# Long convolutions' first stage as two 64-row matmuls into neighbouring banks, PSUM as four banks and two pairs, gates stored by 128 channels

## The chip, the cores and the metric

The kernel runs on one core of one Trainium2 chip. A core has five engines with an instruction queue each: TensorE (PE, matrix products), VectorE (DVE), ScalarE (ACT), GpSimd (POOL) and SyncE (SP, which here only issues transfers). Products land in PSUM, a small memory of 8 banks; one bank takes 512 float32 values in each of 128 partitions. DVE and ACT read PSUM. Everything else lies in SBUF (on the core) or in DRAM. The metric is the device time of one execution in microseconds, the median of several runs.

## The reference, cut to what matters

One layer over 2048 tokens of width 1024: a projection, half of whose columns go through a Fourier mix and half through a gated long convolution, then an output projection, then a two-layer product with a squared ReLU. The change edits the long convolutions and how PSUM is dealt out to all stages.

```
p   = rmsnorm(x) @ w_in            # 512 Fourier columns, 3 x 512: x1, x2, v
y_f = rmsnorm(Re(FFT2(fourier columns)))
x1, x2, v = short_conv(...)        # three taps along the tokens
z = v
for n, gate in enumerate((x1, x2)):
    z = gate * irfft(rfft(z, 4096) * k_freq[n], 4096)[:2048]  (+ z * long_d[n])
x = x + concat(y_f, rmsnorm(z)) @ w_out
x = x + relu(rmsnorm(x) @ w_fc1)**2 @ w_fc2
out = rmsnorm(x)
```

## The kernel before, in words

The stages follow each other, with a small overlap at the seams.

**Projection** (`project`, L308, in two passes, about 0 to 220 and 220 to 425 us). The first pass makes the gates x1 and x2, the second the Fourier columns and v. For each of 16 token tiles there are two products of 24 matmuls (three per weight tile: each float32 operand is split into a high and a low part, `mm3`, L187), into PSUM tiles `pu0` and `pu1`. DVE and POOL apply the three taps, and `finish` (L392) stores a 128 x 512 tile of a gate in the DRAM array `gates`, laid out [128, 16, 512], one piece of 2 KB per partition. Beside the first pass run `filter_hidden` and `fourier_weights`.

**Fourier mix and filters** (L421 and L471, about 425 to 644 us). DFTs as matmuls; the filters' spectra are stored in DRAM as `spec`.

**Long convolutions** (`hyena`, L606, about 644 to 872 us). Eight blocks: two convolutions of four groups of 128 channels. A 4096-point transform is written as two stages of matmuls with a transpose between them. For a block:
- `first(c)` (L636), eight calls for 16 channels each: two matmuls with 256 columns into one PSUM bank `pz1`. The moving operand zz is [128 rows, 16, 16 channels]; the stationary e1 has two matrices, one per half sp. The e1 matrix of half sp is zero in the 64 rows of the other half. DVE then transposes the bank (128 x 512) into G (`turned`, L416).
- `second(q)` (L645), eight slots q: four matmuls of 128 x 128 into `pz2`. ACT makes a turned copy zs of it, DVE multiplies it by the spectrum (y, L655), POOL multiplies zs by the spectrum (L656), and y and zs are added on POOL or DVE (L657). The spectrum `ks` comes by two transfers of 256 KB per slot (L628), into four buffers.
- `inverse(q)` (L660), three slots later: four matmuls of 128 x 128 with y as the stationary operand, into `pv`; ACT copies it to V.
- `turn(c)` (L668): DVE transposes V into W.
- `gate(q)` (L673), four calls: two matmuls whose outputs are the two halves of one bank's partitions (`pb`), and DVE multiplies it by the gate xg into zz (L679). xg of a block is one transfer of 1 MB (`load`, L619) from `gates`.

A hand-written table sets the order over the slots of block i: `second(q)`; at q = 1 the four gates of block i - 2; the last three inverses and the turns of block i - 1; `inverse(q - 3)`; at q = 3 the load of xg for block i - 1; and at the end of a slot the calls of `first` for block i + 1, by the table `FIRSTS` (two in slots 0 and 1, one in slots 2 to 5). All eight calls for block 0 come ahead of the loop.

**Output projection** (`project_out`, L791, to about 1070 us), **first product** (`fc1`, L994, to about 1725 us) and **second product** (`fc2`, L1110, to the end). The last two use a scheme of seven products m1 to m7 instead of eight; `p1u`, `p1m`, `p1v` and `p2u`, `p2m`, `p2v` are their PSUM tiles. In `fc2`, u, m and v are four tiles each, for four groups of 128 tokens; a group of 14 steps is repeated four times for each of two token blocks, and u lives through a whole group.

**PSUM.** All stages take tiles of one bank from `pa` (L165), eight buffers under one tag. A tile's buffer is given out again when every reader of the tile is done. The framework orders the instructions of every engine from the program's order, priorities and an estimate of durations at compile time, and adds the waits; on the chip each engine's order is fixed.

Of the kernel before, what the change touches and what calls it, by code (L numbers as in the profile page):

```python
# [10 lines left out]
F32 = mybir.dt.float32  # L11
# [116 lines left out]
P = 128  # L128
# [6 lines left out]
def hybrid_block(ctx: ExitStack, tc: tile.TileContext, A, out):  # L135
# [7 lines left out]

    gd = [scratch(f"gates{i}", [P, NT, 512]) for i in range(3)]
    kd = [[scratch(f"spec{i}{n}", [P, 32, 128]) for n in range(2)] for i in range(4)]
# [16 lines left out]
    def pool(name, side="left"):  # L162
        return tc.tile_pool(name=name, bufs=1, side=side, reuse_waits="tile")

    def pa(nm):  # L165
        return ps.tile([P, 512], F32, tag="a", name=nm, bufs=8)

# [51 lines left out]
    def transposed(src, nm):  # L219

        for b in (0, 4):
            pt = pa(f"pt_{nm}")
# [7 lines left out]
    def fourier_weights(wp):  # L230

        yield
        rd = load(wp, "rd", [P, P], A["rdft"])
        wt = {}
        for k in range(9):
            if k < 8:
                t = load(wp, "wf", [P, 512], A["w_in"][128 * k : 128 * k + 128, 0:512], 2)
                p = pa("pwt")
                for c in range(4):
                    nc.tensor.transpose(p[:, 128 * c : 128 * c + 128], t[:, 128 * c : 128 * c + 128], ident)  # L240
                wt[k] = wp.tile([P, 4, 128], F32, tag="wt", name="wt", bufs=2)
                nc.scalar.copy(wt[k], p.rearrange("p (c d) -> p c d", c=4))
            if k:
                p = pa("pwr")
                for c in range(4):
                    nc.tensor.matmul(p[:, 128 * c : 128 * c + 128], lhsT=wt[k - 1][:, c, :], rhs=rd, start=True, stop=True)
                wr = wp.tile([P, 512], F32, tag="wr", name="wr", bufs=2)
                nc.scalar.mul(wr, p, gmix[:, k - 1 : k])
                nc.sync.dma_start(wfd[128 * k - 128 : 128 * k, :], wr)
            yield  # L250


    def filter_hidden(fh):

        yield
        w0 = load(fh, "w0", [66, P], A["filt_w0"])
        wi = load(fh, "wi", [P, 2, P], A["filt_wi"])
        fb = load(fh, "fb", [P, 4], A["filt_bf"])
        for half in range(2):
            cur = {}  # L260
            for layer in range(3):
                for q in (2 * half, 2 * half + 1):
                    if layer == 0:
                        cur[q] = load(fh, "feat", [66, 512], A["feat"][:, 512 * q : 512 * q + 512], 2)
                    p = pa(f"ph{layer}")
# [42 lines left out]
    def project(ip, fx, cps, sets, uf):  # L308
# [36 lines left out]
        for i, t in enumerate(order):  # L345
            xh, xl = ahead
            if w is None:
# [9 lines left out]
                if uf is None:  # L357
                    norm(15, xts[15])
            r = rx[t]
            for h, s in enumerate(sets):  # L360
                p = pa(f"pu{h}")
                for k in range(8):
# [29 lines left out]
                def finish(acc, m, tt):  # L392
                    nc.vector.tensor_add(acc, acc, m)
                    nc.sync.dma_start(gd[s][:, tt, :], acc)

# [19 lines left out]

    def turned(dst, c, src):  # L416

        nc.vector.transpose(dst.rearrange("p c f e -> p c e f")[:, 8 * c : 8 * c + 8], src)

# [186 lines left out]
    def hyena(hp, wp, rp, zz, e1, b1, f2, a2, out_weights, out_ahead):  # L606
# [6 lines left out]
        class Block:  # L613
# [5 lines left out]
            def load(self):  # L619
                self.xg = hp.tile([P, NT, 128], F32, tag="xg", name="xg", bufs=2)  # L620
                nc.sync.dma_start(self.xg, gd[1 + self.n][:, :, self.cs])

# [13 lines left out]
            def first(self, c):  # L636
                if c == 0:
                    self.G = big("G")
                p = pa("pz1")
                lo = 128 * self.ct + 16 * c  # L640
                for sp in range(2):
                    nc.tensor.matmul(p[:, 256 * sp : 256 * sp + 256], lhsT=e1[:, sp, :], rhs=zz[:, :, lo : lo + 16], start=True, stop=True)
                turned(self.G, c, p.rearrange("p (l c e) -> p c e l", c=8, e=2))

            def second(self, q):  # L645
                ks = self.ahead if q == 0 and self.ahead else self.spectrum(q)
                p = pa("pz2")
                for j in range(4):
# [11 lines left out]
            def inverse(self, q):  # L660
                if q == 0:
                    self.V = big("V")
                p = pa("pv")
                for j in range(4):
# [8 lines left out]
            def gate(self, q):  # L673
                p = pa("pb")
                for sp in range(2):
# [9 lines left out]
        LAST = ((0,), (1, 2), (3, 4), (5, 6), (7,))  # L685
        FIRSTS = ((0, 1), (2, 3), (4,), (5,), (6,), (7,), (), ())
        blocks = [Block(n, ct) for n in range(2) for ct in range(4)]
        for c in range(8):
            blocks[0].first(c)
# [42 lines left out]
    class Out:  # L732
# [24 lines left out]
        def parts(self, yn, yh, yl, t=0):  # L757

            pt = pa("pt_y")
            for k in range(4):  # L760
# [11 lines left out]
        def ahead(self, hp):  # L772
# [11 lines left out]
            for t, f in zip(tokens, fronts):  # L784
                self.begun[t] = [pa("po") for _ in range(2)]
                for h in range(2):
# [4 lines left out]
    def project_out(op, work, rp, b):  # L791
# [27 lines left out]
        def back(t, f, z):  # L819
            xt = op.tile([P, 1024], F32, tag="oxt", name="oxt", bufs=2)  # L820
            nc.sync.dma_start(xt, x_t[:, t, :])
            x2 = op.tile([P, 1024], F32, tag="ox2", name="ox2", bufs=2)
            for h in range(2):
                if f:
                    p = pa("po")
                    work.multiply(p, f, 0, h)
                else:
                    p = work.begun[t][h]
                cols = slice(512 * h, 512 * h + 512)
# [29 lines left out]
        for i in range(NT + 1):  # L859
# [17 lines left out]
            else:  # L877

                begun = [pa("p1u"), pa("p1m")]
                for p, n in zip(begun, ("m1", "m2")):  # L880
# [22 lines left out]
        for n in ("m5", "m6"):  # L903
            fc1_split(b, n, nc.gpsimd)
        begun.append(pa("p1v"))
        begun.extend([pa("p1u"), pa("p1m")])
        fc1_product(begun[3], ahead["m1"], b["m1"], True)
# [86 lines left out]
    def fc1(mp, rp, zp, b, first, following, begun):  # L994
# [64 lines left out]
        for i in range(33):  # L1059
# [6 lines left out]
            if i < 32:  # L1066
                a = nxt
                if i < 31:
                    nxt = weights(*(fc1_weights(rp, (i + 1) % 16, 1 - i % 2) if i else following), i + 1)
                pu, pm = (pa("p1u"), pa("p1m")) if i > 1 else begun[3 * i : 3 * i + 2]  # L1070
                use(pu, a, "m1", True, i)
# [13 lines left out]
            if i < 32:  # L1085
                use(pu, a, "m6", False, i)
                with tc.high_priority(offset=0 if i else 400):
                    u2 = keep(pu, "ku2")
                pv = pa("p1v") if i else begun[2]
                use(pv, a, "m5", True, i)  # L1090
# [7 lines left out]
        for i, n in enumerate(("m1", "m2")):  # L1098
            parts = []
            for j, v in enumerate(fc2_rows(0, n, 0)):  # L1100
# [3 lines left out]
                split(*parts[j], t)  # L1104
            fc2_begun[n] = [pa("p2" + "um"[i]) for _ in range(4)]
            for j, p in enumerate(fc2_begun[n]):
# [3 lines left out]
    def fc2(mp, blk, gfin, begun):  # L1110
# [64 lines left out]
        def use(k, j):  # L1175
            g, n, e = steps[k]
            bank, start, (rows, cols) = todo[n]
            if k in parts:
                if start and e == 0:
                    held[bank, j] = pa(f"p2{bank}")  # L1180
                fc2_product(held[bank, j], j, *parts[k], start and e == 0)
# [195 lines left out]
```

## Time and profile before

| | |
|---|---|
| median of 3 runs | 2336.13 us (2333.21 to 2342.69) |
| the profiled execution's own time | 2342.11 us |
| its span, from the first to the last instruction | 2340.2 us |
| mean granted TensorE clock | 0.986 |
| PE busy, whole span | 2247.7 us |
| stretch 0 to 220 us (first projection pass): PE busy | 209.02 us |
| 220 to 425 (second pass): PE busy | 191.45 us |
| 425 to 644 (Fourier mix, filters): PE busy, DVE busy | 196.12 us, 186.80 us |
| 644 to 872 (long convolutions): PE busy, DVE busy, DMA share | 211.54 us, 173.16 us, 0.89 |
| 872 to 1070 (output projection): PE busy | 195.08 us |
| 1070 to 1725 (first product): PE busy | 638.77 us |
| 1725 to 2340 (second product): PE busy, DVE busy | 605.74 us, 427.36 us |

"Busy" is the time in which an engine runs at least one instruction. The ends of matmuls are modelled, so a busy PE need not be at its peak. A row of a timeline gives start, duration, engine, line, operation, output tile and input tiles, and how many records were merged; a float32 matmul leaves two records, since it is run in two passes. In brackets stands the idle time before it, and who ended it. "DMA share" is the mean busy share of the core's 16 DMA engines; a value a little over 1 means that packets overlap on an engine.

### The profile page before, as it was taken

To read this page: it belongs to the slowest core of one execution; us is meant where nothing else is said; L and a number is where in the kernel's file an instruction comes from. 1 tells how busy PE (TensorE), PEld (TensorE's weight loads), DVE (VectorE), ACT (ScalarE), POOL (GpSimd) and SP (SyncE) were. 2 spreads that over 40 slices of the span, in tenths; PEclk is the share of its full clock that TensorE was granted. 3 is DMA by queue.
4 is the path that set the end of the run, shared out by engine and by line. 5 is a ranking of instruction groups with operands and counts; after the bars stand their busy time and mean duration, and the time that the engine had idled before them with its cause. 6 is when DMAs were issued, how large, how long until landed. Compare 5 with 4: busy or idle time off the path is not lost.

```text
span 2340.2 us, 30973 instructions
## 1 busy us (share of the span) xinstructions
PE 2247.7 (96%) x10984; PEld 1861.0 (80%) x10984; DVE 1548.4 (66%) x2284; ACT 1104.3 (47%) x1809; POOL 846.8 (36%) x634
## 2 busy tenths in 40 slices
PE   8999998989899989998999999999999999999998
PEld 6887787788788857886788877888888888888886
DVE  7998666789767874447544456444466666866667
ACT  6554211455455554545655566555543333533334
POOL 4345322566656622216755565555400000000000
PEclk9999999999999989999999999999999999999999
DMA  7535888456688986557544456444479766866631
GB/s 258 178 134 179 304 321 300 139 174 206 227 207 191 212 224 189 176 175 244 162 150 149 152 207 203 153 149 151 151 261 377 238 197 196 280 209 197 192 123 72
DMA packets 294779, 468.41 MB, mean 200 GB/s; under 512 B 18453, under 2 KB 142687, under 8 KB 290273
## 3 DMA queue, kind: packets, MB, share of 16 engines
q1 hardware_dynamic: 291265, 460.43, 61.5%
q10 hardware_dynamic: 3360, 6.02, 0.8%
q8 instruction: 86, 1.41, 0.3%
q14 instruction: 68, 0.56, 0.1%
HBM read 312.54 MB, written 152.27 MB: 199 GB/s over the span
## 4 chain that ended last, share of the span: by engine, by line
PE 73%; DMA 9%; DVE 9%; ACT 3%; POOL 3%; issue 2%; SPq 1%; ACTq 0%; DVEq 0%; POOLq 0%
PE p2u L190 5%; PE p2u L189 5%; PE p2u L191 5%; PE p1u L191 5%; PE p1u L189 5%; PE p1u L190 4%; DMA ks<-spec 3%; PE pu L191 3%; PE pu L190 3%; PE pu L189 3%; PE p2v L189 2%; PE p2v L190 2%; PE p2v L191 2%; DMA f<-in_w_fc 2%; PE p1v L189 2%; PE p1v L191 2%
## 5 line engine op out<-in xcount | busy, mean ns | idle before, releaser
L181 ACT CAST qahm<-ra 128x1024 fp32r<-128x1024 f32 x110 | 115.9, 1053 | 345.9 <-PE p2u L190 172.0
L182 DVE TENSOR_TENSOR qalm<-ra,qahm 128x1024 fp32r<-128x1024 f32 x110 | 134.7, 1225 | 155.5 <-ACT qahm L181 151.8
L1159 POOL TENSOR_TENSOR acc<-acc,gfin 128x512 f32<-128x512 f32 x4 | 5.1, 1279 | 633.1 <-DMA out<-acc 625.9
L189 PE MATMUL pu<-wh,xh 128*128 128x512 f32 x512 | 205.7, 403 | 8.9 <-ACT wh L184 5.5
L190 PE MATMUL pu<-wl,xh 128*128 128x512 f32 x512 | 202.6, 396 | 6.5 <-DVE wl L182 3.7
L191 PE MATMUL pu<-wh,xl 128*128 128x512 f32 x512 | 203.0, 397 | 2.7 <-DVE xl L182 2.7
L190 PE MATMUL p2u<-qblm,qahm 128*128 128x512 f32 x504 | 196.2, 389 | 0.5 <-DVE qblm L182 0.5
L189 PE MATMUL p2u<-qbhm,qahm 128*128 128x512 f32 x504 | 195.9, 389 | 0.1
L191 PE MATMUL p2u<-qbhm,qalm 128*128 128x512 f32 x504 | 195.8, 389 | 0.0
L182 DVE TENSOR_TENSOR qblm<-rb,qbhm 128x1024 fp32r<-128x1024 f32 x110 | 134.1, 1219 | 1.4 <-ACT qbhm L181 1.1
L397 POOL TENSOR_TENSOR acc<-acc,cw 128x512 f32<-128x512 f32 x45 | 60.8, 1351 | 202.8 <-DVE acc L374 201.4
L189 PEld LDWEIGHTS pu<-wh,xh 128*128 128x128 f32 x512 | 98.1, 192 | 31.1 <-ACT wh L184 7.0
L181 ACT CAST ahm<-s 128x512 fp32r<-128x512 f32 x124 | 76.6, 620 | 95.3 <-PE p1v L190 55.2
L190 PEld LDWEIGHTS pu<-wl,xh 128*128 128x128 f32 x512 | 98.0, 191 | 28.9 <-DVE wl L182 4.1
L182 POOL TENSOR_TENSOR alm<-W,ahm 128x512 fp32r<-128x512 f32 x63 | 85.9, 1364 | 94.2 <-ACT ahm L181 94.2
L181 ACT CAST qbhm<-rb 128x1024 fp32r<-128x1024 f32 x110 | 115.3, 1049 | 5.0 <-DMA a1m<-c 2.9
L191 PEld LDWEIGHTS pu<-wh,xl 128*128 128x128 f32 x512 | 97.8, 191 | 24.1 <-DVE xl L182 3.6
L189 PEld LDWEIGHTS p2u<-qbhm,qahm 128*128 128x128 f32 x504 | 94.5, 188 | 20.6 <-ACT qbhm L181 0.5
L190 PEld LDWEIGHTS p2u<-qblm,qahm 128*128 128x128 f32 x504 | 94.6, 188 | 20.3 <-DVE qblm L182 1.0
L191 PEld LDWEIGHTS p2u<-qbhm,qalm 128*128 128x128 f32 x504 | 94.6, 188 | 19.8
L191 PE MATMUL p1u<-bm,alm 128*128 128x512 f32 x252 | 100.1, 397 | 6.4 <-DVE alm L182 6.4
L189 PE MATMUL p1u<-bm,ahm 128*128 128x512 f32 x252 | 100.2, 397 | 6.2 <-ACT ku L1022 6.2
(380 smaller groups left out, 6445.4 us busy)
## 6 DMA issues: line engine op xcount, KB each, us to landing
W<-in_w_fc SPq DMA_DIRECT2D x66, 512.0 KB, 4.4
ks<-spec SPq DMA_DIRECT2D x128, 256.0 KB, 6.8
rb<-td SPq DMA_DIRECT2D x64, 512.0 KB, 4.5
ra<-a1m SPq DMA_DIRECT2D x56, 512.0 KB
ra<-a0m SPq DMA_DIRECT2D x54, 512.0 KB, 10.7
rb<-in_w_fc SPq DMA_DIRECT2D x46, 512.0 KB, 4.5
f<-in_w_fc SPq DMA_DIRECT2D x16, 1024.0 KB
td<-f SPq DMA_DIRECT2D x16, 1024.0 KB, 5.0
```

What stands on the lines that cost most here:

```text
L181: nc.scalar.copy(hi, src)
L182: (eng or nc.vector).tensor_sub(lo, src, hi)
L189: nc.tensor.matmul(o, lhsT=lh, rhs=rh, start=start, stop=False, skip_group_check=more)
L190: nc.tensor.matmul(o, lhsT=lh, rhs=rl, start=False, stop=False, skip_group_check=more)
L191: nc.tensor.matmul(o, lhsT=ll, rhs=rh, start=False, stop=stop, skip_group_check=more)
L397: nc.gpsimd.tensor_add(m1, m1, cw[:, 3, :])
L1159: nc.gpsimd.tensor_mul(acc[i][:, c], acc[i][:, c], gfin[:, c])
```

## The change

Three parts.

First, `first(c)` works on 32 channels instead of 16. Each of its two matmuls takes only the 64 rows in which its matrix is not zero, has 512 columns, and writes a bank of its own; the two banks are one PSUM tile `pz`, and DVE transposes 128 x 1024 at once. There are four calls per block, in slots 0, 1, 3 and 5.

Second, PSUM is split into a tag of four single banks (`pb`) and a tag of two pairs (`pz`, `halves`). Second stage, inverse and gates take single banks. The projection's two products, the output projection's, u and m of the first product, and m and v of the second take the halves of a pair; v of the first product and u of the second take single banks. The Fourier mix and the filters still call `pa`, which now gives out four single banks and then the halves of two pairs, in turn.

Third, the gates x1 and x2 lie in DRAM as [128, 4, 16, 128]: the store of a tile has four pieces of 512 bytes per partition, and the load of xg has one piece of 8 KB per partition instead of 16 pieces of 512 bytes.

```diff
-    gd = [scratch(f"gates{i}", [P, NT, 512]) for i in range(3)]
+    gd = [scratch(f"gates{i}", [P, 4, NT, 128] if i else [P, NT, 512]) for i in range(3)]
...
+    def pb(nm):
+        return ps.tile([P, 512], F32, tag="a", name=nm, bufs=4)
+
+    def pz(nm):
+        return ps.tile([P, 1024], F32, tag="z", name=nm, bufs=2)
+
+    def halves(nm):
+        z = pz(nm)
+        return [z[:, 0:512], z[:, 512:1024]]
+
+    turns = []
+
     def pa(nm):
-        return ps.tile([P, 512], F32, tag="a", name=nm, bufs=8)
+        if not turns:
+            turns.extend([None] * 4 + [0, 1, 0, 1])
+        k = turns.pop(0)
+        if k is None:
+            return pb(nm)
+        if k == 0:
+            pa.pair = halves(nm)
+        return pa.pair[k]
...
+            pair = halves("pu")
             for h, s in enumerate(sets):
-                p = pa(f"pu{h}")
+                p = pair[h]
...
-                    nc.sync.dma_start(gd[s][:, tt, :], acc)
+                    if s:
+                        nc.sync.dma_start(gd[s][:, :, tt], acc.rearrange("p (c j) -> p c j", c=4))
+                    else:
+                        nc.sync.dma_start(gd[s][:, tt, :], acc)
...
-    def turned(dst, c, src):
+    def turned(dst, c, src, n=8):
-        nc.vector.transpose(dst.rearrange("p c f e -> p c e f")[:, 8 * c : 8 * c + 8], src)
+        nc.vector.transpose(dst.rearrange("p c f e -> p c e f")[:, n * c : n * c + n], src)
...
-                nc.sync.dma_start(self.xg, gd[1 + self.n][:, :, self.cs])
+                nc.sync.dma_start(self.xg, gd[1 + self.n][:, self.ct])
...
-                p = pa("pz1")
-                lo = 128 * self.ct + 16 * c
+                p = pz("pz1")
+                lo = 128 * self.ct + 32 * c
                 for sp in range(2):
-                    nc.tensor.matmul(p[:, 256 * sp : 256 * sp + 256], lhsT=e1[:, sp, :], rhs=zz[:, :, lo : lo + 16], start=True, stop=True)
-                turned(self.G, c, p.rearrange("p (l c e) -> p c e l", c=8, e=2))
+                    h = slice(64 * sp, 64 * sp + 64)
+                    nc.tensor.matmul(p[:, 512 * sp : 512 * sp + 512], lhsT=e1[h, sp, :], rhs=zz[h, :, lo : lo + 32], start=True, stop=True)
+                turned(self.G, c, p.rearrange("p (l c e) -> p c e l", c=16, e=2), 16)
...
-                p = pa("pz2")
+                p = pb("pz2")
...
-                p = pa("pv")
+                p = pb("pv")
...
-                p = pa("pb")
+                p = pb("pb")
...
-        FIRSTS = ((0, 1), (2, 3), (4,), (5,), (6,), (7,), (), ())
+        FIRSTS = ((0,), (1,), (), (2,), (), (3,), (), ())
...
-        for c in range(8):
+        for c in range(4):
             blocks[0].first(c)
...
-                self.begun[t] = [pa("po") for _ in range(2)]
+                self.begun[t] = halves("po")
...
-                pu, pm = (pa("p1u"), pa("p1m")) if i > 1 else begun[3 * i : 3 * i + 2]
+                pu, pm = halves("p1u") if i > 1 else begun[3 * i : 3 * i + 2]
...
-            fc2_begun[n] = [pa("p2" + "um"[i]) for _ in range(4)]
+            fc2_begun[n] = halves("p2m") + halves("p2m") if i else [pb("p2u") for _ in range(4)]
...
-                    held[bank, j] = pa(f"p2{bank}")
+                    if bank == "u":
+                        held[bank, j] = pb("p2u")
+                    elif j % 2 == 0:
+                        held[bank, j], held[bank, j + 1] = halves(f"p2{bank}")
```

More of the change, by code (lines that the diff above doesn't have):

```diff
@@ L221, in transposed @@
         for b in (0, 4):
-            pt = pa(f"pt_{nm}")
+            pt = pb(f"pt_{nm}")
             for k in range(4):
@@ L237, in fourier_weights @@
                 t = load(wp, "wf", [P, 512], A["w_in"][128 * k : 128 * k + 128, 0:512], 2)
-                p = pa("pwt")
+                p = pb("pwt")
                 for c in range(4):
@@ L243, in fourier_weights @@
             if k:
-                p = pa("pwr")
+                p = pb("pwr")
                 for c in range(4):
@@ L264, in filter_hidden @@
                         cur[q] = load(fh, "feat", [66, 512], A["feat"][:, 512 * q : 512 * q + 512], 2)
-                    p = pa(f"ph{layer}")
+                    p = pb(f"ph{layer}")
                     nc.tensor.matmul(p, lhsT=w0 if layer == 0 else wi[:, layer - 1, :], rhs=cur[q], start=True, stop=True)
@@ L757, in parts @@
         def parts(self, yn, yh, yl, t=0):
-            pt = pa("pt_y")
+            pt = pb("pt_y")
             for k in range(4):
@@ L822, in back @@
             x2 = op.tile([P, 1024], F32, tag="ox2", name="ox2", bufs=2)
+            pair = halves("po") if f else work.begun[t]
             for h in range(2):
+                p = pair[h]
                 if f:
-                    p = pa("po")
                     work.multiply(p, f, 0, h)
-                else:
-                    p = work.begun[t][h]
                 cols = slice(512 * h, 512 * h + 512)
@@ L877, in project_out @@
             else:
-                begun = [pa("p1u"), pa("p1m")]
+                begun = halves("p1u")
                 for p, n in zip(begun, ("m1", "m2")):
@@ L904, in project_out @@
             fc1_split(b, n, nc.gpsimd)
-        begun.append(pa("p1v"))
-        begun.extend([pa("p1u"), pa("p1m")])
+        begun.append(pb("p1v"))
+        begun.extend(halves("p1u"))
         fc1_product(begun[3], ahead["m1"], b["m1"], True)
@@ L1088, in fc1 @@
                     u2 = keep(pu, "ku2")
-                pv = pa("p1v") if i else begun[2]
+                pv = pb("p1v") if i else begun[2]
                 use(pv, a, "m5", True, i)
```

## Prediction

> **What bounds the kernel now.** I read the page first, then the busy time by stretch, then the chain of waits, and last the timeline of the long convolutions, since the change edits their first stage.
>
> ```profile
> span 2340.2 us, 30973 instructions
> PE 2247.7 (96%) x10984; PEld 1861.0 (80%) x10984; DVE 1548.4 (66%) x2284; ACT 1104.3 (47%) x1809; POOL 846.8 (36%) x634
> ...
> PE 73%; DMA 9%; DVE 9%; ACT 3%; POOL 3%; issue 2%; SPq 1%; ACTq 0%; DVEq 0%; POOLq 0%
> ```
>
> PE is the bound as a whole: 96% busy, and 73% of the chain that ends last. So microseconds taken from PE count, unless something else in their stage is late next. The stage concerned lasts from 644 to 872 us. The next rows are two stretches in it (PE, weight loads, DVE, ACT, POOL busy; granted clock; DMA share; GB/s):
>
> ```profile
> 697.90:724.40 26.50, 25.44 (x178) 21.61 (x178) 20.29 (x33) 14.47 (x25) 15.83 (x14) 1.00 0.91 198
> 826.10:872.00 45.90, 34.74 (x189) 23.07 (x189) 35.60 (x62) 24.16 (x41) 12.49 (x10) 0.85 0.86 215
> ```
>
> Two resources are nearly full in the first stretch: PE 25.44 of 26.50 us, DMA 0.91. DVE has 6 us to spare. The chain gives the period of a block, read from one burst of gates to the next (start, us):
>
> ```profile
> 697.94 3.59 PE pb L678 x16
> ...
> 802.92 3.59 PE pb L678 x16
> ```
>
> Four periods in 104.98 us, 26.2 us each. The PE timeline inside a period:
>
> ```profile
> 696.89 1.05 PE L649 MATMUL pz<-G,f 128*128 128x128 f32 x8
> 697.87 3.66 PE L678 MATMUL pb<-W,b 128*64 128x512 f32 x16
> 701.46 1.16 PE L665 MATMUL pv<-y,a 128*128 128x128 f32 x8
> 702.46 1.89 PE L642 MATMUL pz<-zz,e1z 128*128 128x256 f32 x8
> 704.19 1.06 PE L649 MATMUL pz<-G,f 128*128 128x128 f32 x8
> 705.08 1.05 PE L665 MATMUL pv<-y,a 128*128 128x128 f32 x8
> 705.97 1.03 PE L642 MATMUL pz<-zz,e1z 128*128 128x256 f32 x4
> ...
> 716.57 1.06 PE L649 MATMUL pz<-G,f 128*128 128x128 f32 x8
> 718.52 1.13 PE L665 MATMUL pv<-y,a 128*128 128x128 f32 x8 [0.89 <-DVE y L657]
> ```
>
> Start to start, a second stage (L649) and an inverse (L665) cost 0.89 us each, two calls of the first stage (L642, eight matmul records) 1.73, the four gates (L678) 3.59. A block has eight of each of the first three and four gates: 16 x 0.89 + 4 x 1.73 + 3.59 + about 0.3 around the gates = 25.1. The other 1.1 us of the 26.2 are waits like the last row's: the inverse waits for y, which waits for its spectrum's transfer. So PE sets the pace, and the ks transfers stand just behind it.
>
> **The first stage on PE.** It had 128-row matmuls of 256 columns, half of whose rows meet zeros; it gets two matmuls of 64 rows and 512 columns per 32 channels. The rows hold no matmul of 64 rows. The nearest is the gate, which splits the columns of the array: 16 records of 512 columns in 3.59 us, where L642 does 8 of 256 columns in 1.73, so 16 of 512 would be 6.92 one after the other. The gate's halves therefore run side by side, 0.43 us a pair. Around it PE loses time: L649 before it takes 0.98 instead of 0.89, eight pairs take 3.59 instead of 3.46, L665 behind it 1.00 instead of 0.89, together 0.33. If rows split as columns do, a new call costs 2 x 0.43 + 0.33 = 1.2 us against 1.73 for the two old ones that it replaces: 0.54 saved. If they do not overlap, it costs 1.73 + 0.33 = 2.06. I take the overlap, because the gate is the same data type, the same two passes, and half an array. A block saves 4 x 0.54 = 2.1 us of PE; seven blocks run such calls for their successor.
>
> A rule speaks against this. The Trainium skill (TensorE: Matmul & The Clock Gate, Part 3, The mechanism) says that a weight load overlaps a running matmul only where the row group differs; each half's second pass would then wait for its weights. This trace does not bear it out for full-array matmuls (weight loads 80% busy beside matmuls 96%). By the rule a call would show four bare loads of 21.61/178 = 0.12 us each: 1.2 + 0.5 = 1.7, and nothing saved. No row here shows it for half rows.
>
> **Up front**, eight old calls run before any other work of the stage:
>
> ```profile
> 643.96 6.92 PE pz L642 x32
> ...
> 651.68 1.16 PE pz L649 x8
> ...
> L418 DVE STREAM_TRANSPOSE G<-pz 128x512 f32<-128x512 f32 x64 | 44.6, 704 | 19.0 <-PE pz L642 17.7
> L182 DVE TENSOR_TENSOR qalm<-ra,qahm 128x1024 fp32r<-128x1024 f32 x110 | 134.7, 1225 | 155.5 <-ACT qahm L181 151.8
> ```
>
> The new transposes are 128x1024; none is in the trace. Bounds: twice 704 ns, or below that by one fixed cost; the nearest row of that size takes 1225, and I take 1.24 us. Four of them behind the first call: 1.1 + 5.0 = 6.1 us instead of 7.7 (643.96 to 651.68), 1.6 saved, DVE now last. In the blocks DVE loses 0.7 us of work per block; it has room.
>
> **Banks.** This is the cost. The eight banks were one rotation; now second stage, inverse and gates share four, and the first stage has two pairs. What DVE does around a burst of gates:
>
> ```profile
> 699.00 0.69 DVE L679 TENSOR_TENSOR zz<-pb,xg 128x512 f32<-128x512 f32 x1 [0.86 <-PE pb L678]
> ...
> 702.19 1.28 DVE L655 TENSOR_TENSOR y<-pz,ks 128x512 f32<-128x512 f32 x2
> ```
>
> By the order of issue the two second-stage results read at 702.19, behind the four gate products, are those of slots 7 and 0; the result of 696.89 (slot 1) is read later still. So when the gates start at 697.87 three banks are full, and four banks leave one for four gates. The gates then wait on reads. Bounds: nothing, if DVE reads the two results before the gates; and one gate per bank, 697.87 to 699.69 = 1.82 us each, so 3 x 1.82 + 0.9 = 6.4 instead of 3.59, 2.8 lost. The order of DVE follows the banks, so the two reads should move up as soon as their spectra are there: I take 0.9 a block, for the first bank turning once alone.
>
> **Gates by channels and the ks transfers.** The load of xg (1 MB, issued once a block ahead of four ks loads) goes from 512-byte pieces to 8 KB ones.
>
> ```profile
> 245.00:425.00 180.00, 173.10 (x752) 140.77 (x751) 114.13 (x142) 29.16 (x36) 52.48 (x34) 0.99 0.81 294
> 700.50:704.30 3.80, 3.80 (x23) 2.77 (x20) 3.46 (x7) 0.64 (x1) 2.43 (x3) 1.00 0.03 10
> 707.00:710.00 3.00, 3.00 (x26) 2.90 (x25) 2.88 (x5) 1.88 (x4) 2.04 (x2) 1.00 1.18 283
> 712.00:725.00 13.00, 11.94 (x90) 10.87 (x90) 9.07 (x15) 8.02 (x14) 6.15 (x6) 1.00 1.07 227
> ```
>
> ```profile
> xg<-gates SPq DMA_DIRECT2D x8, 1024.0 KB, 8.9
> ```
>
> From 707 to 710 xg moves at 283 GB/s, 3.7 us for its 1.05 MB; from 712 on ks moves at 227, 2.3 us per 512 KB, without a gap; around the gates (700.5 to 704.3) nothing moves, since ks buffers are held by the two late reads. In the stretch with large pieces the engines reach 294 GB/s at a share of 0.81, so 363 at full share: xg would take 2.9 us, and the ks behind it land 0.8 us earlier (bounds: nothing, and 2.7, if a bad spread over the engines goes as well). I take 1.5. PE reaches the waiting inverse of 718.52 earlier too: from the burst to it six old calls (5.2 us) become three new ones (3.6), plus 0.9 for the banks, so 0.7 earlier; the wait of 0.89 shrinks to almost nothing, and a later one takes about 0.6.
>
> Stores of these gates get four pieces per row instead of one, all in the first 220 us; on SP's queue they stand ahead of loads of x, but DMA is busy at 0.56 there, so I count nothing. Bounds: a gain has no reason; at 0.3 us more issue for 32 stores up to 3 us of cover would go.
>
> ```profile
> 0.00:220.00 220.00, 209.02 (x987) 170.37 (x988) 187.78 (x327) 122.53 (x194) 93.33 (x75) 0.99 0.56 188
> ```
>
> **Banks elsewhere.** In the last matrix product u has exactly four single banks, so its next group waits for the reads of the previous one. It matters where the token block changes, where DVE is late:
>
> ```profile
> 2025.82 0.68 DVE L1188 TENSOR_TENSOR acc<-acc,p2u 128x512 f32<-128x512 f32 x1
> ...
> 2031.93 0.67 DVE L1188 TENSOR_TENSOR acc<-acc,p2u 128x512 f32<-128x512 f32 x1
> ```
>
> ```profile
> 1725.00:2340.00 615.00, 605.74 (x2669) 500.12 (x2667) 427.36 (x543) 242.46 (x274) 5.12 (x4) 0.99 0.64 215
> ```
>
> A product is six matmuls of 605.74/2669 us, 1.36. The third result was complete by 2025.82, the fourth by 2027.2, and the new block's fourth product would start three products on, at 2031.3; its bank is read until 2032.6. Up to 1.3 us plus restart, taken as 1.5; nothing if PE's order is changed around it. In the other stages pairs come back two products later at least, and I count nothing.
>
> **The sum.** A block in the middle: 26.2 - 2.1 (PE) + 0.9 (banks) - 0.4 (ks) = 24.6, so 1.6 less, four times: -6.4. Block 6 (6 old calls to 3 new, with gates): -0.7. Block 0 (no gates): -2.1. Block 1: -1.5. Up front -1.6. The tail of block 7, where DMA alone is behind: -1.5 by xg. Token block: +1.5. Together -12.3. The profiled execution took 2342.1 (span 2340.2 and 1.9 around it), 6 above the median of the three runs; the difference holds for either, so from 2336.1 the forecast is 2324. Its own range is 2318 to 2329.
>
> **Rivals.** (a) *PE alone sets the blocks.* DVE's reads and ks arrive in time: period 25.1 - 2.1 = 23.0, so -3.2 four times, -1.6, -2.1, -2, -1.6, -2.5: 2313. For it: DMA needs only 8 x 2.3 + 2.9 = 21.3 a block. Against: three full banks at the gates.
> (b) *The ks wait takes the gain.* xg is no quicker in effect, and the inverse waits as before; only the one call after that wait is saved: -0.5 four times, and with -0.3, -2.1, -1, -1.6, +1.5 about 2331. For it: DMA at 1.07 for 13 us on end.
> (c) *Slower: the four banks go round in turn.* Each second stage then waits until the result two slots back is read. The read of 702.19 would hold back the second stage of 696.89 by up to 6 us, 3 if DVE is prompt; with 4 the period is 29, +2.8 four times, +2.9 in block 6, -2.1, -1.6, and +3.3 at the token block with its restart: 2350. It decides from 1.6 us of extra wait a block on. For it: the reads follow transfers that land late in every block.
> (d) *The halves do not overlap* (one after the other at 2.06 a call; bare weight loads between them, 1.7, would stay below that): at 2.06, +1.3 a block with +0.9 for banks less 1.1 for ks: +1.1 four times, +1.8, +1.3, +1.3, 0 up front, -1.5, +1.5: 2345.
>
> **How the numbers follow.** Forecast 0.44, (a) 0.18, (b) 0.14, (c) 0.14, (d) 0.10. A measurement can tell about 0.5%, 11.7 us, from no change: below 2324.4 is faster, above 2347.8 slower. Faster: a bit over half of the forecast's share (0.25), all of (a), a trace of (b): 0.44. Slower: most of (c) and a third of (d): 0.13. The rest, 0.43, is within. The range leaves out half of (a) and about half of (c): 2313 to 2348.
>
> **What would show it.** Pairs of first-stage records starting together and about 0.43 us from the next pair; a call at about 1.2 us; periods between gates of 24 to 25 us; gates a little longer than 3.59; xg landing well below 8.9 us; transposes of 1.24 us. I am wrong if the call takes 2 us, if second stages wait for the reads of y, or if the gates stretch to 6 us; and if PE has new waits outside 644 to 872, the bank edits cost where I counted nothing.

## The result, and the profile after

| | before | after |
|---|---|---|
| median | 2339.41 us (2333.21 to 2345.64, 4 runs) | 2397.64 us (2395.81 to 2399.57, 4 runs) |
| profiled execution | 2342.11 us | 2398.21 us |

The ratio is 1.0249 (95% interval 1.0217 to 1.0281): the change costs 58 us. The prediction was 2324, and its range ended at 2348.

The page of the changed kernel: span, busy time by engine, one row of its DMA issues (to landing, us).

```profile
span 2396.4 us, 30718 instructions
...
PE 2267.4 (95%) x10856; PEld 1822.9 (76%) x10856; DVE 1547.1 (65%) x2252; ACT 1105.4 (46%) x1807; POOL 853.2 (36%) x634
...
xg<-gates SPq DMA_DIRECT2D x8, 1024.0 KB, 9.6
```

The span grew by 56 us, PE's busy time by only 20, although PE has 128 matmul records fewer. So it is mostly waiting that came in, not work. (The ends of matmuls are modelled: behind the last matmul before a stop, a part of the stop counts as busy.) Where? I cut both traces at the start of the last matmul into pu, pk and pb, of the first into p1u and p2u, and of the last of the second product, beginning with PE's first instruction (us):

| | projection | Fourier mix, filters | long convolutions | output projection | first product | second product |
|---|---|---|---|---|---|---|
| before | 416.5 | 222.7 | 226.9 | 208.3 | 635.9 | 616.1 |
| after | 432.1 | 234.1 | 249.6 | 211.9 | 634.1 | 620.5 |
| difference | +15.6 | +11.4 | +22.7 | +3.7 | -1.8 | +4.4 |

More than half of the loss lies outside the stage that I had costed.

**Projection.** PE's waits in the projection of the changed kernel (us in total, times, longest):

```profile
PE pu L211 <- DVE m L397: 6.7, 5, 3.3
...
PE pu L211 <- ACT uf L391: 4.2, 3, 2.6
PE pu L211 <- ACT full L403: 2.7, 2, 2.1
```

The rows with m, uf and full are new: the first matmul of a tile waits until DVE or ACT has read an older tile, 13.6 us in all. Before, PE waited here only for operands and loads. Some of those waits got shorter (wh 0.5 us instead of 5.5, wl 0.9 instead of 6.4), so all rows of this view together grew by only 4 us, and 11 of the stage's 15.6 count as busy. From start to start the stops show: between two matmuls into pu the median is 0.227 us in both traces, but 124 of these distances are over 0.3 us now, 76 before, and they hold 13 us more beyond the median. Eight tiles of depth had become two pairs, and each pair comes free only when both products have been read.

**Filters.** The same view for this stage. The row is its longest and is new: generating the next filter waits until ACT has copied an older spectrum out of its bank. Other rows changed too, by 4 us and less.

```profile
PE pk L522 <- ACT ks L582: 6.0, 5, 2.1
```

**Long convolutions.** One period on PE, from one burst of gates to the next:

```profile
758.05 1.08 PE L706 MATMUL pb<-W,b 128*64 128x512 f32 x4
759.92 1.08 PE L706 MATMUL pb<-W,b 128*64 128x512 f32 x4 [0.79 <-DVE zz L707]
761.79 1.08 PE L706 MATMUL pb<-W,b 128*64 128x512 f32 x4 [0.80 <-DVE zz L707]
763.67 1.08 PE L706 MATMUL pb<-W,b 128*64 128x512 f32 x4 [0.80 <-DVE zz L707]
764.68 1.16 PE L693 MATMUL pv<-y,a 128*128 128x128 f32 x8
...
773.68 1.12 PE L670 MATMUL pz<-zz,e1z 64*128 64x512 f32 x2
774.73 1.16 PE L677 MATMUL pz<-G,f 128*128 128x128 f32 x8
...
776.72 1.12 PE L670 MATMUL pz<-zz,e1z 64*128 64x512 f32 x2
777.88 1.16 PE L677 MATMUL pz<-G,f 128*128 128x128 f32 x8
778.97 1.13 PE L670 MATMUL pz<-zz,e1z 64*128 64x512 f32 x4
780.39 1.13 PE L670 MATMUL pz<-zz,e1z 64*128 64x512 f32 x4 [0.28 <-DVE G L444]
782.11 1.12 PE L670 MATMUL pz<-zz,e1z 64*128 64x512 f32 x2 [0.60 <-DVE G L444]
783.17 1.16 PE L693 MATMUL pv<-y,a 128*128 128x128 f32 x8
784.25 1.12 PE L670 MATMUL pz<-zz,e1z 64*128 64x512 f32 x2
785.31 1.16 PE L677 MATMUL pz<-G,f 128*128 128x128 f32 x8
...
788.38 1.08 PE L706 MATMUL pb<-W,b 128*64 128x512 f32 x4
```

The period is 30.3 us (758.05 to 788.38), not 26.2. Two things show. The gates come one at a time, 1.87 us apart, so a burst lasts 6.63 us (758.05 to 764.68) instead of 3.59. And of the four first-stage calls two are torn apart: a row "x2" is one half (two records), and between the halves of 773.68 and 776.72 stand a second stage and an inverse. A half alone takes 1.05 us from its start to the next instruction; a whole call, "x4", takes hardly more. So the first stage costs 7.5 us a block (1.05 + 1.16 + 4.20 + 1.06) instead of 6.9 before. The remaining 0.5 of the added 4.1 lies around the sixteen other steps. Over the whole stage PE's waits are these, first the longest one of before, then those of the changed kernel:

```profile
PE pv L665 <- DVE y L657: 10.2, 14, 2.8
```

```profile
PE pb L706 <- DVE zz L707: 13.5, 17, 0.8
PE pz L670 <- DVE G L444: 5.1, 11, 0.6
PE pz L677 <- ACT V L694: 4.7, 5, 1.1
...
PE pv L693 <- DVE y L685: 2.7, 4, 1.5
PE pv L693 <- ACT V L694: 2.4, 7, 0.7
PE pv L693 <- DVE y L683: 2.2, 1, 2.2
```

The rows with V are new as well: V is no operand of these matmuls, so they wait until ACT has read an inverse's result out of the bank that they need. The four single banks hold up second stages and inverses too, by 7.1 us in all.

Why do the gates wait? What DVE and POOL do at the next burst:

```profile
789.51 0.69 DVE L707 TENSOR_TENSOR zz<-pb,xg 128x512 f32<-128x512 f32 x1 [1.48 <-PE pb L706]
791.38 0.69 DVE L707 TENSOR_TENSOR zz<-pb,xg 128x512 f32<-128x512 f32 x1 [1.18 <-PE pb L706]
793.26 0.69 DVE L707 TENSOR_TENSOR zz<-pb,xg 128x512 f32<-128x512 f32 x1 [1.18 <-PE pb L706]
793.87 1.28 DVE L683 TENSOR_TENSOR y<-pz,ks 128x512 f32<-128x512 f32 x2
...
795.66 0.68 DVE L707 TENSOR_TENSOR zz<-pb,xg 128x512 f32<-128x512 f32 x1
796.26 0.68 DVE L683 TENSOR_TENSOR y<-pz,ks 128x512 f32<-128x512 f32 x1
```

```profile
790.25 2.51 POOL L684 TENSOR_TENSOR zs<-zs,ks 128x512 f32<-128x512 f32 x2
```

Three second-stage results (read at 793.87 and 796.26) fill three of the four single banks. POOL multiplies by the spectra of the first two from 790.25 on, so those had landed; DVE stood idle 1.18 us before each of the gates of 791.38 and 793.26, and a read takes 0.64 (1.28 for two). It did not read because its order, fixed at compile time, has three gates first. (The first gate of this burst could still start at once; in five of the eight bursts, all four come one at a time in 6.63 us.)

### The profile page after: what moved, and what is told of

Read it like the earlier page. It is cut to its first block, busy times and chain, and to the rows that moved or that the text cites. A ratio compares the mean times of both kernels' runs of the same rounds, so it can differ in the third digit from the quotient of the medians.

```text
span 2396.4 us, 30718 instructions
## 1 busy us (share of the span) xinstructions
PE 2267.4 (95%) x10856; PEld 1822.9 (76%) x10856; DVE 1547.1 (65%) x2252; ACT 1105.4 (46%) x1807; POOL 853.2 (36%) x634
## 4 chain that ended last, share of the span: by engine, by line
PE 61%; DVE 7%; ACT 3%; DMA 3%; issue 2%; POOL 2%; SPq 1%; DVEq 0%; ACTq 0%; POOLq 0%
PE p1u L211 6%; PE p1u L213 5%; PE p1u L212 5%; PE p2u L212 5%; PE p2u L213 5%; PE p2u L211 5%; PE p2v L211 2%; PE p2v L212 2%; PE p2v L213 2%; PE p1v L211 2%; PE p1v L213 2%; PE p1v L212 2%; PE po L211 2%; PE po L212 2%; PE po L213 2%
## 5 line engine op out<-in xcount | busy, mean ns | idle before, releaser
L211 PEld LDWEIGHTS p2u<-qbhm,qahm 128*128 128x128 f32 x504 | 94.5, 188 | 21.4 <-DVE acc L1218 1.7
L204 POOL TENSOR_TENSOR alm<-s,ahm 128x512 fp32r<-128x512 f32 x62 | 94.7, 1528 | 25.6 <-ACT ahm L203 25.6
```

The source lines that it names most:

```text
L204: (eng or nc.vector).tensor_sub(lo, src, hi)
L211: nc.tensor.matmul(o, lhsT=lh, rhs=rh, start=start, stop=False, skip_group_check=more)
```

## The experiments

My theory after the trace: the PSUM split makes the loss, in three ways (stages ahead short of tiles, gates one at a time, halves torn apart); the 64-row form itself gains and the gates' storage does nothing. The rival: the new form or the storage carries much of it. Differences by stage are those of the profiled executions against that of before, cut as above; ratios are against the kernel before, run beside them (medians 2335.3 to 2335.6). The profiled execution of before took 2342.1 us, above these medians, and gates_alone differs from it by -2.5 in the output projection, which it leaves alone: in one stage of one run, 3 to 4 us say little.

| kernel | median us | ratio (95%) | projection | Fourier mix, filters | long conv. | output proj. | first product | second product |
|---|---|---|---|---|---|---|---|---|
| banks_alone | 2402.82 | 1.0296 (1.0265 to 1.0328) | +12.4 | +12.6 | +25.3 | +4.2 | -0.9 | +4.6 |
| gates_undone | 2397.94 | 1.0276 (1.0249 to 1.0303) | +14.5 | +14.9 | +23.7 | +3.3 | -1.5 | +4.3 |
| pu_in_turn | 2393.86 | 1.0259 (1.0229 to 1.0289) | +8.9 | +13.0 | +22.0 | +1.3 | -2.6 | +3.5 |
| six_and_pair | 2379.04 | 1.0198 (1.0170 to 1.0226) | +22.1 | +4.9 | +7.5 | +0.1 | -0.1 | -0.3 |
| split_late_four | 2371.44 | 1.0156 (1.0141 to 1.0171) | 0.0 | -1.7 | +21.5 | +6.0 | -0.7 | +4.0 |
| halves_400 | 2387.03 | 1.0228 (1.0213 to 1.0243) | +15.1 | +14.8 | +8.5 | +5.6 | -0.3 | +4.6 |
| split_late_six | 2346.45 | 1.0048 (1.0031 to 1.0064) | -0.8 | +0.1 | +6.7 | +2.7 | -3.1 | -0.2 |
| late_six_60 | 2355.45 | 1.0090 (1.0075 to 1.0105) | +0.1 | -0.6 | +16.6 | +0.5 | -3.3 | -0.1 |
| late_four_400 | 2359.51 | 1.0105 (1.0088 to 1.0123) | +1.2 | +0.3 | +12.6 | +1.7 | -0.8 | +4.2 |
| late_gp_100 | 2375.51 | 1.0171 (1.0152 to 1.0189) | -1.2 | -0.4 | +28.0 | +2.4 | -2.0 | +5.5 |
| one_gate_bank | 2371.53 | 1.0146 (1.0120 to 1.0171) | -0.8 | -0.4 | +35.7 | -1.9 | +0.1 | -0.6 |
| gates_alone | 2334.37 | 0.9991 (0.9980 to 1.0003) | -0.9 | 0.0 | -3.9 | -2.5 | -0.3 | -0.3 |

### Which part costs: the split alone

```diff
-                p = pz("pz1")
+                if c % 2 == 0:
+                    self.pair = halves("pz1")
+                p = self.pair[c % 2]
...
+                    nc.tensor.matmul(p[:, 256 * sp : 256 * sp + 256], lhsT=e1[:, sp, :], rhs=zz[:, :, lo : lo + 16], start=True, stop=True)
```

> The changed kernel with only the PSUM split kept: four single banks and two pairs as in the change, but the first stage again as eight calls of 128 rows (two calls share a pair, one bank each) and the gates stored as before. Theory 1 (the split alone makes the loss): the second projection pass keeps its 15 us, Fourier mix and filters 11, the second product 5, and the gates still come one per bank, 6.6 us instead of 3.6 in seven blocks, 21 us; together 50 to 58 us over the kernel before, so 2385 to 2398. Theory 2 (the 64-row calls and the new storage of the gates carry much of the loss): at most 30 us over the kernel before, 2370 or less.

Measured 2402.8, 67 us over the kernel before, and above the expected 2385 to 2398: the split alone makes the whole loss. The next kernel, run beside it, has the 64-row form and the same split and storage, and is 62.5 us over the kernel before. The 4.9 us between the two lie within the scatter (2397.5 to 2408.1 and 2395.2 to 2401.4), so a gain by the form as it stands in the changed kernel is not shown.

### The storage of the gates, undone and alone

```diff
-                nc.sync.dma_start(self.xg, gd[1 + self.n][:, self.ct])
+                nc.sync.dma_start(self.xg, gd[1 + self.n][:, :, self.cs])
```

> The changed kernel with only the gates' storage put back (512 values per row and tile in one piece, the load of xg in 512-byte pieces). Theory 1 (the split alone makes the loss): the time of the changed kernel within 4 us, 2394 to 2402, with xg landing about as late as with the 8 KB pieces. Theory 2 (stores in four pieces hold up loads in the first projection pass, or the large pieces of xg fill few engines): 2385 or less.

> The kernel before with only the gates' storage by 128 channels. Theory (transfers of xg are not what a block waits for, and the smaller pieces of the stores are covered): the time of the kernel before within 4 us. Rival (the ks transfers behind xg land earlier and shorten the waits for y): 5 to 10 us faster.

Undone: 2397.9, as the changed kernel (2397.64). Alone: 0.9991 with an interval that holds 1. The row of gates_undone, with the 512-byte pieces of xg:

```profile
xg<-gates SPq DMA_DIRECT2D x8, 1024.0 KB, 8.7
```

The 8 KB pieces land no sooner: 9.6 us in the changed kernel and 9.3 in gates_alone, against 8.7 here, 8.9 before and 9.7 in banks_alone. So the storage is worth nothing that can be measured, and the 1.5 us by which ks was to land earlier were wrong.

### The projection's tiles in turn

```diff
-            pair = halves("pu")
...
-                p = pair[h]
+                p = pa(f"pu{h}")
```

> The changed kernel, but the projection's two products take tiles from the four single banks and the two pairs in turn, eight tiles deep, instead of the halves of one pair, four tiles deep. Theory 1 (the second projection pass loses its 15 us because two pairs hold only two token tiles ahead): 12 to 16 us less than the changed kernel, 2382 to 2386. Rival (the pass loses time by the order of its instructions or by its transfers, whatever the tiles): within 4 us of the changed kernel.

Measured 2393.9: 4 less, not 12 to 16, and so the rival's number. The projection fell by 6.7 us only, and that in the fastest of the four executions (2388.1; the others took 2393.5 to 2394.5). Its waits:

```profile
PE pu L211 <- ACT xh L203: 8.9, 3, 6.9
...
PE pu L211 <- DVE m L396: 1.7, 3, 0.8
PE pu L211 <- ACT uf L390: 1.6, 2, 0.8
```

The waits for readers are nearly gone (3.5 us with the short ones, from 13.6), as the theory says; but a late operand, xh, takes 8.9 us, 6.9 of them at once, behind a load of x that stands late in SP's order: it was issued at 329.55 us, 23 us after the one before it, and xh was made from it at 336.2. The wait was exchanged for another.

### Six single banks and one pair

```diff
-        return ps.tile([P, 512], F32, tag="a", name=nm, bufs=4)
+        return ps.tile([P, 512], F32, tag="a", name=nm, bufs=6)
...
-        return ps.tile([P, 1024], F32, tag="z", name=nm, bufs=2)
+        return ps.tile([P, 1024], F32, tag="z", name=nm, bufs=1)
```

> The changed kernel with PSUM as six single banks and one pair: first stage in the pair, everything else in single banks or in all eight in turn, v and m of the second product two single banks and the pair. Theory 1 (depth of the split is the cause): gates come together again, 3.6 us a burst, the projection and the filters are back at the times of before, and 64-row calls save up to 2 us in seven blocks: 2320 to 2340. Rival (pairs and 64-row calls cost by themselves, in whatever split): 2365 or more.

Measured 2379, a miss of 2320 to 2340 and the rival's number: the long convolutions fell to +7.5 and the filters to +4.9, but the projection rose to +22.1, again with waits for operands behind late loads of x (xh 8.8, xl 7.2 us in the second pass). Depth alone does not explain the projection; what the split does to the order of its instructions counts too.

### The split only from the long convolutions on

```diff
+    early_ps.close()
+    cur[:] = [ctx.enter_context(tc.tile_pool(name="ps", bufs=2, space=PSUM, reuse_waits="tile")), False]
     with pool("raws") as rp:
```

> PSUM is eight single banks in one rotation for the projection, the Fourier mix and the filters, and is split into four single banks and two pairs only from the long convolutions on; all else as in the changed kernel. Theory (the stages ahead of the long convolutions lose only by the split, through the order of instructions that it leads to): their 27 us come back, 18 in the projection and 9 to 12 in Fourier mix and filters, and the long convolutions keep their 20 to 23: 2366 to 2374. Rival (these stages lose by the stores of 512 bytes, or by chance of transfer times): 2385 or more.

Measured 2371.4, as expected. With eight single banks in one rotation, projection and filters are back at their times (0.0 and -1.7). The split, and nothing else of the change, had cost them 27 us by the traces, 26 by the medians. (The new pools also carry the flag reuse_waits="tile", which the changed kernel's pool doesn't have; the long convolutions, under the same flag, keep their +21.5.)

> As the kernel with the late split, but with six single banks and one pair from the long convolutions on. Theory (depth of single banks decides the gates): bursts of 3.6 us, the long convolutions 10 us over the kernel before at most (one pair makes bunched first-stage calls wait for each other's transpose), all else as before: 2340 to 2350. Rival (the late split brings nothing at the stages ahead): 2370 or more.

Measured 2346.5, as expected. Its gates on PE:

```profile
781.40 3.66 PE L713 MATMUL pb<-W,b 128*64 128x512 f32 x16
785.00 1.16 PE L700 MATMUL pv<-y,a 128*128 128x128 f32 x8
```

Four gates in 3.6 us again, and 25 us less than with four and two. The long convolutions are still 6.7 us over the kernel before. Their waits now:

```profile
PE pz L677 <- DVE G L451: 9.5, 7, 1.4
PE pv L700 <- DVE y L692: 8.2, 12, 2.2
```

The first row is the price of one pair: a call waits for the transpose of the one before.

> As the kernel with six single banks and one pair from the long convolutions on, and the first-stage matmuls moved up by 60 places of the program's order, which spreads them over a block. Theory (calls that follow each other at once wait for the one pair, 1.25 us of transpose each): 5 to 10 us less than without the move, 2332 to 2342, about the kernel before. Rival (the calls wait for the pair anyway, or push the second stages back): the same time as without the move, within 3 us.

Measured 2355.5, a miss of both: moved up, the calls waited for the pair 12.7 us instead of 9.5, 7 calls of 32 are torn apart instead of 4, and the long convolutions lost 10 us more. The second stages have most of it, 81.0 us instead of 75.1, each counted to the next start on PE; why is not shown. The order that I had taken for better was worse.

### The halves kept together

```diff
+                with tc.high_priority(offset=400):
                     for sp in range(2):
```

> The changed kernel with the two 64-row matmuls of every first-stage call kept next to each other in TensorE's order (both moved up by 400 places of the program's order). In the changed kernel 12 of 32 calls have other work between the halves, and each half then takes 1.05 us, as much as a whole call. Theory (lone halves eat the gain of the 64-row form): first-stage calls take 1.06 us each, 2 to 2.5 us less in each of seven blocks; with the gates still one at a time, 8 to 18 us less than the changed kernel: 2380 to 2390. Rival (only the gates and waits behind them matter; a call moved up just waits elsewhere): within 4 us of the changed kernel.

Measured 2387, 11 us less than the changed kernel. A burst of gates and two calls behind it:

```profile
783.95 1.08 PE L706 MATMUL pb<-W,b 128*64 128x512 f32 x4
...
789.57 1.16 PE L693 MATMUL pv<-y,a 128*128 128x128 f32 x8
...
791.33 1.99 PE L670 MATMUL pz<-zz,e1z 64*128 64x512 f32 x8
```

Two whole calls take 2 us, and no call is torn. From the start of a first-stage matmul to the next start on PE, all of them take 36 us, against 53 in the changed kernel and 56 before; a part of that goes into other waits, since the whole kernel gains only 11. The gates here get a bank sooner (783.95 to 789.57, 5.62 us a burst), so not all of the 11 us is due to the halves.

> Two of the causes removed at once: eight single banks until the filters are done (split into four banks and two pairs only from the long convolutions on), and the two halves of each first-stage call next to each other (moved up by 400 places). Theory (the causes add): 27 us for the stages ahead and 11 for the lone halves less than the changed kernel's 2398, so 2357 to 2364; what is left over the kernel before lies in the gate bursts (5 to 6.6 us instead of 3.6) and the stages behind. Rival (what one removal wins, the other had won already): 2368 or more.

Measured 2359.5, as expected: 27 us for the stages ahead and 11 for the order of the calls add up.

### Other banks for the gates

```diff
-                p = pb("pb")
+                if q % 2 == 0:
+                    self.pp = halves("pb")
+                p = self.pp[q % 2]
```

> As the kernel with the late split into four banks and two pairs, but the gates take the halves of the pairs instead of single banks, and the first-stage matmuls are moved up by 100 places. Theory (gates come one at a time because three of the four single banks hold second-stage results not yet read): TensorE no longer waits for the reads of gate products, 13.5 us in the changed kernel, under 3 here, and the calls keep together: 2335 to 2350. Rival (the read by VectorE sets the 1.87 us a gate, whatever the bank): the waits for these reads stay at 10 us or more in all, 2355 or more.

Measured 2375.5, a miss in the time, and 4 us more than the late split with the gates in single banks (2371.4). The waits for reads of gate products fell, nearly as the theory says, from 13.5 us to 3.4:

```profile
PE pb L714 <- DVE nw_s L229: 5.9, 1, 5.9
PE pb L714 <- DVE zz L715: 3.4, 2, 2.6
```

But the last block's gates wait once for 5.9 us, and the column halves of 16 of the 32 gates are torn apart:

```profile
774.71 1.07 PE L714 MATMUL pb<-W,b 128*64 128x512 f32 x2
775.71 1.16 PE L683 MATMUL pz<-G,f 128*128 128x128 f32 x8
...
777.69 1.07 PE L714 MATMUL pb<-W,b 128*64 128x512 f32 x2
```

Half a gate alone takes 1.00 us (774.71 to 775.71); a whole gate in a burst takes 0.90 (3.59 / 4). How the loss divides between the torn gates and the rest, this trace does not show.

```diff
+    def pg(nm):
+        return ps.tile([P, 512], F32, tag="g", name=nm, bufs=1)
...
-                p = pa("pb")
+                p = pg("pb")
```

> The kernel before, with seven banks in rotation and one bank for the gates alone (v and m of the second product put their fourth tile there). First stage, gates' storage and all else as before. The order of instructions then puts other stages between the gates. Theory (one bank at a time costs the changed kernel 3 us a block only because everything else on TensorE wants the same four banks): at most 1 us a block lost, 2335 to 2345. Rival (one bank for four gates costs 3 us a block in itself): 2352 or more.

Measured 2371.5: the rival's number, 36 us over the kernel before. But the place differs from what it says: PE's waits for reads of gate products are 7.1 us, and the inverses wait for y 21.4 us instead of 10.2:

```profile
PE pv L668 <- DVE y L660: 21.4, 15, 4.8
PE pb L681 <- DVE zz L682: 7.1, 9, 0.8
```

Spread among the other steps, the gates delay the making of y on DVE: in one burst DVE stands idle 2.98 us for a gate's product (read at 749.80), only then multiplies the next second-stage result (750.41) and adds (751.20), and the inverse starts at 752.92 after 1.29 us of waiting. A third wait, of 6.0 us, comes once, ahead of the last block's gates. So seven free banks for the rest do not help when gates have one.

No version with the 64-row calls beats the kernel before. The nearest, split_late_six, is 0.48% slower. Both halves in one bank, which would need no pairs, was not tried: the Trainium skill (TensorEngine Tiling (Array Packing), Restrictions and Gotchas) says that different row tiles cannot access the same PSUM bank at the same time. No run here shows it.

## Why the prediction was wrong, step by step

The sum had about -13.8 us for the long convolutions and +1.5 for the token block; the traces have +22.7 and, everywhere else, +33.3. A block in the middle was to take 24.6 us and took 30.3. Two signs that the prediction had named as signs of being wrong came: gates stretched to 6.6 us, and new waits outside 644 to 872.

**The first stage on PE: right while the halves stand together.** Up front and between two blocks (changed kernel):

```profile
671.13 1.99 PE L670 MATMUL pz<-zz,e1z 64*128 64x512 f32 x8
...
677.23 2.05 PE L677 MATMUL pz<-G,f 128*128 128x128 f32 x16
679.21 1.13 PE L670 MATMUL pz<-zz,e1z 64*128 64x512 f32 x4
680.27 2.05 PE L677 MATMUL pz<-G,f 128*128 128x128 f32 x16
```

A call takes 1.06 us (679.21 to 680.27); I had 1.2, and rival (d) 2.06. Up front took 6.1 us (671.13 to 677.23), as forecast. The transposes took 1.24 us, as taken:

```profile
L444 DVE STREAM_TRANSPOSE G<-pz 128x1024 f32<-128x1024 f32 x32 | 39.5, 1241 | 33.0 <-PE pz L677 17.9 <-PE pz L670 14.8
```

What failed is what I never priced: that the two halves follow each other. The -2.1 us a block became +0.6, since 12 of the 32 calls are torn apart and bunched calls wait for pairs (the row with "DVE G", 5.1 us in all). By the rule of the Trainium skill that I weighed (TensorE: Matmul & The Clock Gate, Part 3, The mechanism) a call would take 1.7; this trace has 1.06. That is 2 x 0.53, 0.1 a pass more than the 0.43 of a pair, which would fit, as an estimate, one uncovered load of weights (0.12) a pass for both halves at once, and not four in a row; the rows do not settle it.

**Banks at the gates: the size failed.** "I take 0.9 a block" on the ground that "the two reads should move up". They did not: DVE's order put three gates first. The upper bound was 2.8, at 1.82 us a gate; measured were 3.0, at 1.87. I named the right mechanism and chose the wrong end. Whether the reads come first was set by the compiler's order, and the only row of it that I had, the reads at 702.19, stood behind the gates: that was a reason to take the upper bound for the forecast, not the lower third. The waits of second stages and inverses for banks (the rows with V, 7.1 us) had no term in the sum.

**Banks elsewhere: the step failed.** "In the other stages pairs come back two products later at least, and I count nothing." I looked only at when a pair comes round, not at who reads it: a tile of the projection is read by DVE for up to three taps, or by ACT, and the next tile then stood 13.6 us in all behind these reads. The split cost 27 us there and in the filters (split_late_four), and the second product shows +4.4 (3.5 to 5.5 in every kernel with four single banks there, nothing in the others). The output projection's +3.7 is less sure: 1.3 to 6.0 with four single banks, -2.5 to 2.7 without. The wait at the token block, taken as 1.5, was there: PE waited 1.3 us for acc (L1218). The other 3 us of the second product are open; with six singles and a pair they are gone.

**The gates' storage and ks: the step failed.** xg landed after 9.6 us, not well below 8.9; worth 0 instead of 0.4 to 1.5. The stores cost nothing, as counted. The waits for y fell from 10.2 us to 5.1 in the long convolutions (rows with y; in one of them, 2.2 us, the wait ends with the multiplication that also frees a bank). The storage is not the cause, since gates_undone has 6.3; that PE, held up at the gates, comes later is my reading of it.

**Rivals.** (c), the four banks in turn, had the sign, and its period of 29 was near the 30.3; but it put the wait at the second stages, where the rows have 4.7 us in all (pz, ACT V), and the gates have 13.5. At 2350 it lacked the 27 us ahead of the stage. Its chance of 0.14 was too low: the three full banks stood in the rows.

**What stays open.** In the projection I can't divide the loss between waits for readers and loads of x that came late in SP's order: both appear, and taking one away brought the other (pu_in_turn, six_and_pair).

## What to carry to other kernels

A rotation of eight banks is also a reserve that lets the compiler's order run ahead; cutting it into classes has a price in every stage that shares it, so measure the cut alone, and make it only for the stage that needs it. Two matmuls that gain by running side by side gain only next to each other in the engine's order: look there, not only in the program. And where a wait depends on an order that is set at compile time, forecast with the worse bound.

## What the runs showed of the hardware

- Two float32 matmuls of 64 rows and 512 columns into two banks take 1.06 us together, one alone 1.05. The same holds for column halves: 1.00 alone, 0.90 a pair in a burst, and 1.01 a pair that stands alone (one_gate_bank, 754.87 to 755.88).
- Through one bank, matmul, read by DVE and the next matmul make a cycle of 1.87 us for a gate: PE stands idle for 0.8 of it, and the read of 0.69 lies in that time.
- Pieces of 8 KB instead of 512 bytes did not make a 1 MB load beside other loads land sooner: 9.3 and 9.6 us against 8.7, 8.9 and 9.7.
